# A feed-forward layer in fp32: seven-product schemes moved from every pair of its second product to all of the first and half of the second

## The chip, the core and the metric

The kernel runs on one core of a Trainium2 chip. The metric is the device time of one execution in microseconds (us); of several runs the median is taken. Five engines matter: TensorE (PE, matrix products, which accumulate in eight banks of PSUM), VectorE (DVE), ScalarE (ACT) and GpSimd (POOL) for elementwise work, and SyncE (SP), whose queue issues every DMA of this kernel in the order in which the program gives them.

## The reference, cut to what matters

One decoder layer on 1024 tokens of width 1024: attention and RWKV mixing, then the MLP that the change rewrites, then a gated embedding. Of the MLP:

```python
f = rmsnorm(h, ffn_pre_norm[i])                                   # 1024 x 1024
f = jnp.square(jax.nn.relu(f @ w_ff_in[i])) @ w_ff_out[i]         # 1024 x 4096, then 1024 x 1024
h = h + rmsnorm(f, ffn_post_norm[i])
```

## The kernel before, in words

**Numbers.** All is fp32. TensorE works on operands split in two parts: `hi` is the value rounded by a ScalarE copy to the type fp32r, `lo` is the remainder, made by a subtraction on VectorE or GpSimd. `mm3` (L289) makes each product from three matmuls, hi·hi, hi·lo and lo·hi, each with 128 rows of contraction, 128 output rows and 512 output columns. Every operand thus costs one ScalarE copy and one subtraction, each on 128x512 or 128x1024 elements.

**Order.** PE's instructions are written in the order that a planner (`Order`, L136) works out at build time: it keeps a planned time for each engine, interleaves the dense work with "chains" of dependent work (`spawn`), and so fixes PE's order. SP's order is the program's own within the MLP (`manual_schedule` at L1587). The order on VectorE, ScalarE and GpSimd is there left to the framework's scheduler, but each engine then works its queue in that order: an instruction that waits holds up those behind it. Named buffers (`rtile`, L455, and `mtile`, L1237) have a fixed place by a tag, such as `kk` or `BK2`; a new tile of a tag waits until the last reader of the old one is done.

**Before the MLP.** `out_0` and `out_1` (L1346, L1364) are the product with w_out, eight token blocks each; each `out_1(i)` spawns a chain `mixed(i)` (L1409), which normalises the token block, transposes it on PE (`tr`, tile `tp`) and stores it, split, as operand of the MLP (`put_T`, L1391; tile `f`). The MLP's first product may read tokens 0 to 511 once `mixed(3)` is done, and tokens 512 to 1023 once `mixed(7)` is done.

**First product** (1024x1024 by 1024x4096), before: plain. The 4096 hidden columns are 32 chunks `j` of 128; a chunk has two halves of 512 tokens; a half takes 8 steps of contraction, three matmuls each, into one bank `z` (`ff1_half`, L1450), then Relu and Square on ScalarE (`ff1_evac`, L1454) into `raw_h[p]` (tile `hr`), p = j // 2. Three of the halves for the first 512 tokens run while `mixed(7)` is still under way (`ff1_first`, L1627). The weights of a chunk come by one DMA of 512 KB, one copy and one GpSimd subtraction of 128x1024 (`wload`, L313).

**Second product** (1024x4096 by 4096x1024), before: the 4096 rows of contraction are 16 pairs p of two blocks of 128. For 15 of them, the pair's product is seen as 2x2 blocks by 2x2 blocks (blocks of contraction, token halves, output halves) and made with seven products of blocks instead of eight, in the manner of Strassen and Winograd. `operands` (L1499) makes the sums and differences on GpSimd, from `raw_h` (tile `sum`) and from the weights `w2r` (tile `ws`); `split2` (L1491) splits them into tiles `duo`; `prep(n)` (L1530) calls both, two products ahead; `product(n)` (L1540) makes four groups of three matmuls in banks `bk`, and after each group VectorE adds the bank to the running total `tot`, which is 28 additions in a pair. `ff1(j)` (L1583) interleaves: 12 matmuls of the first product, then one product of the second. The last pair is made plainly at the end (`last_split`, L1464, and `ff2_last`, L1649), with weights that were split early and come back by DMA (`lw`, `lwl`). `part` (L1564) uses the time between to split later weights and to put them in DRAM (`gp`, `pkg`).

## Time and profile before

| what | value |
|---|---|
| median of 3 runs (lowest, highest) | 1776.96 us (1774.38, 1780.42) |
| the profiled execution's own time | 1773.19 us |
| its span, first to last instruction | 1771.4 us |
| MLP, from the first matmul on `f` to the first on `lw` | 982.41 to 1626.10 us |
| TensorE's mean granted clock | 0.999 |

The profile shows one execution: 1.8 us of its time lie outside the span. PE's busy time counts matmuls that overlap in the array, so a matmul's duration (0.39 us) is longer than the step from one to the next. A row of a group gives its line, engine, operation, the tile written and those read, the shape, the count, the busy sum, the mean of one in ns, and the idle time of the engine just ahead of these instructions with what ended it. Nearly all elementwise work has line 113, a helper, so that tiles tell the groups apart, and all DMA issues have line 132.

### The profile page before, as it was taken

What the parts mean: (1) busy time and instruction counts of PE and PEld (TensorE: products, weight loads), DVE (VectorE), ACT (ScalarE), POOL (GpSimd) and SP (SyncE); (2) the same over time, 40 slices, a digit from 0 to 9 for tenths busy, and PEclk for the clock granted to TensorE, in tenths of its full rate; (3) what the DMA queues carried; (4) which work ended last, traced back from release to release, by engine and by line L of the source; (5) the groups of instructions that cost most, each with busy time, mean ns of one, the idle gap of its engine ahead of it and who ended that gap; (6) DMA issues with size and microseconds to landing.
All of it is one profiled execution on the core that took longest, in us unless ns stands there. A gap on an engine that the chain in (4) does not pass through costs nothing.

```text
span 1771.4 us, 25935 instructions
## 1 busy us (share of the span) xinstructions
PE 1743.8 (98%) x10192; PEld 1423.4 (80%) x10192; DVE 1017.1 (57%) x1834; ACT 732.3 (41%) x1315; POOL 670.5 (38%) x423
## 2 busy tenths in 40 slices
PE   9999989999999999999999999999999999999998
PEld 8787877878877777778888878888788888888887
DVE  6289777776534233353735466665666566556643
ACT  5824343432344343542434434343334334333454
POOL 1344131231232323332230266666665566652311
PEclk9999999999999999999999999999999999999999
DMA  4621121212332222333524132332232232305611
GB/s 163 211 95 37 49 78 47 98 43 96 86 134 84 60 60 72 110 111 135 201 96 139 64 113 95 94 115 87 92 118 91 84 95 90 123 9 179 214 48 48
DMA packets 67132, 175.51 MB, mean 99 GB/s; under 512 B 7745, under 2 KB 8129, under 8 KB 66498
## 3 DMA queue, kind: packets, MB, share of 16 engines
q1 hardware_dynamic: 67010, 173.86, 29.6%
q8 instruction: 80, 1.31, 0.3%
q14 instruction: 42, 0.34, 0.1%
HBM read 125.20 MB, written 41.94 MB: 94 GB/s over the span
## 4 chain that ended last, share of the span: by engine, by line
PE 82%; DVE 5%; DMA 5%; ACT 3%; POOL 2%; issue 2%; SPq 0%; DVEq 0%; ACTq 0%; POOLq 0%
PE z L294 18%; PE z L296 18%; PE z L292 18%; PE bk L292 6%; PE bk L294 5%; PE bk L296 5%; PE sc L275 1%; DVE xy L113 1%; PE y L275 1%; PE po L275 1%; PE pt L283 1%; PE A L275 1%; PE wr L275 1%; PE fq L275 1%; POOL wl L113 1%
## 5 line engine op out<-in xcount | busy, mean ns | idle before, releaser
L113 POOL TENSOR_TENSOR wl<-wr,wh 128x1024 fp32r<-128x1024 f32 (+1 forms) x87 | 208.0, 2392 | 431.4 <-ACT wh L113 412.2
L113 DVE TENSOR_TENSOR tot<-tot,bk 128x512 f32<-128x512 f32 x420 | 272.7, 682 | 129.9 <-PE bk L296 129.7
L292 PE MATMUL z<-uh,wh 128*128 128x512 f32 (+1 forms) x800 | 312.3, 390 | 5.5 <-ACT part L113 3.0
L296 PE MATMUL z<-uh,wl 128*128 128x512 f32 (+1 forms) x800 | 312.6, 391 | 2.7 <-POOL wl L113 2.7
L294 PE MATMUL z<-ul,wh 128*128 128x512 f32 (+1 forms) x800 | 313.6, 392 | 1.3 <-DVE ul L113 1.3
L292 PE MATMUL z<-f,wh 128*128 128x512 f32 x496 | 193.2, 389 | 0.3 <-ACT f L113 0.3
L294 PE MATMUL z<-f,wh 128*128 128x512 f32 x496 | 193.1, 389 | 0.2 <-DVE f L113 0.2
L296 PE MATMUL z<-f,wl 128*128 128x512 f32 x496 | 193.0, 389 | 0.0
L292 PEld LDWEIGHTS z<-uh,wh 128*128 128x128 f32 x800 | 151.1, 189 | 36.2 <-ACT part L113 3.5
L296 PEld LDWEIGHTS z<-uh,wl 128*128 128x128 f32 x800 | 151.0, 189 | 34.1 <-POOL wl L113 4.0
L294 PEld LDWEIGHTS z<-ul,wh 128*128 128x128 f32 x800 | 151.2, 189 | 32.3 <-issue 3.6
L292 PE MATMUL bk<-duo 128*128 128x512 f32 x420 | 164.3, 391 | 4.0 <-DVE tot L113 3.9
L294 PE MATMUL bk<-duo 128*128 128x512 f32 x420 | 163.5, 389 | 0.0
L296 PE MATMUL bk<-duo 128*128 128x512 f32 x420 | 163.5, 389 | 0.0
L113 ACT ACTIVATE wh<-wr 128x1024 fp32r<-128x1024 f32 (+1 forms) x87 | 90.3, 1038 | 119.0 <-PE z L294 89.8
L113 POOL TENSOR_TENSOR duo<-w2r,duo 128x512 fp32r<-128x512 f32 x45 | 66.7, 1483 | 166.0 <-ACT duo L113 166.0
L113 POOL TENSOR_TENSOR duo<-ws,duo 128x512 fp32r<-128x512 f32 x60 | 81.0, 1350 | 122.3 <-ACT duo L113 119.0
L292 PEld LDWEIGHTS z<-f,wh 128*128 128x128 f32 x496 | 93.1, 188 | 20.0 <-ACT f L113 0.5
L294 PEld LDWEIGHTS z<-f,wh 128*128 128x128 f32 x496 | 93.1, 188 | 19.8 <-DVE f L113 0.5
L296 PEld LDWEIGHTS z<-f,wl 128*128 128x128 f32 x496 | 93.1, 188 | 19.2
L292 PEld LDWEIGHTS bk<-duo 128*128 128x128 f32 x420 | 78.8, 188 | 23.7 <-DVE tot L113 7.0
L296 PEld LDWEIGHTS bk<-duo 128*128 128x128 f32 x420 | 78.8, 188 | 16.4
(312 smaller groups left out, 3203.5 us busy)
## 6 DMA issues: line engine op xcount, KB each, us to landing
wr<-in_wz_dram SPq DMA_DIRECT2D x48, 512.0 KB, 3.7
wr<-in_wff_dram SPq DMA_DIRECT2D x31, 512.0 KB, 3.6
w2r<-in_w_ff_dram SPq DMA_DIRECT2D x30, 512.0 KB, 4.2
xt<-in_x_dram SPq DMA_DIRECT2D x16, 512.0 KB, 4.3
gscr<-gst SPq DMA_DIRECT2D x32, 256.0 KB, 2.0
g<-gscr SPq DMA_DIRECT2D x16, 512.0 KB, 4.2
wpg<-pkg SPq DMA_DIRECT2D x16, 512.0 KB, 6.7
sw<-qk SPq DMA_DIRECT2D x48, 128.0 KB, 2.3
```

The costliest lines, as they stand in the source:

```text
L113: return f(*a, **kw)
L275: PE.matmul(out_, a, b, start=start, stop=stop)
L283: PE.transpose(out_, a, ident if idn is None else idn)
L292: PE.matmul(ps, ah, bh, start=start and i == 0, stop=False, skip_group_check=not start)
L294: PE.matmul(ps, ah, bl, start=False, stop=False, skip_group_check=not start)
L296: PE.matmul(ps, al, bh, start=False, stop=i == n - 1, skip_group_check=not start)
```

## The change

**First product: sevens everywhere.** Contraction halves by token halves, and a pair of 128-column chunks, form the 2x2 blocks. Seven products per pair, each four steps of contraction (12 matmuls, `w1_mm`), replace four chunk halves of 24 matmuls. The operand sums on the token side are made once, in `put_f` (tiles `F[1]` to `F[7]`, for tokens 512 to 1023 six POOL operations in a block where there were none). The sums of weights are made for each pair on GpSimd (`w1_sum`, four), after 256 KB loads (`w1_raw`).

**Two of the seven made first.** Products 1 and 2 of a pair need only the first 512 tokens. All 32 of them (`early`) come ahead: 27 before anything that needs tokens 512 to 1023, five interleaved with pair 0. Their results go to DRAM (`p1_scr`, `c_scr`) and come back with four 256 KB loads for each pair (`take`). The other five (`SEQ`, function `first`) accumulate in two banks `z`, taken in turn; VectorE adds the bank to `raw_h`.

**Second product: sevens for even pairs only.** `seven` is the old `product` with a new order (`MUL`); `plain` makes odd pairs with eight products, where both blocks of contraction add up in the bank (six matmuls for each VectorE addition, 16 additions in a pair). In even pairs the operand sums of `raw_h` move from GpSimd to VectorE, and the subtractions of their splits from VectorE to GpSimd. The four sums of weights for an even pair are made and split during the odd pair before (`w2_sums`), written to DRAM (`bs_scr`, 512 KB each) and loaded again in `prep`.

**Order and rooms.** Subtractions are put off by a few matmuls (`pend`, `flush`). Between products of the second stand 2 or 3 `chunks` of three matmuls of the first. Buffers change tags: `tot` lies in the old place of `f`, three tags rotate for `w2r`, and the late loads (`e_weights`, `last_split`, `last_weights`) come at other points of the last pair.

```diff
+        yield from put_f(hh, i)
...
+    def put_f(srcs, i):
...
+        if i == 4:
+            for n, p, h in ((3, 0, 0), (7, 1, 0), (5, 0, 1), (6, 1, 1)):
+                t = mtile("hl"[p], h, [128, 2, 4, 512], "f", F32R)
+                F[n] = t[:, 0], t[:, 1]
+            F[4] = [rtile([128, 4, 512], "f", tag, F32R) for tag in ("AR0", "AR1")]
...
+                S.activation(at(1 + b, 0), ps, AF.Copy)
+                V.tensor_tensor(at(1 + b, 1), ps, at(1 + b, 0), OP.subtract)
...
+        t2, t4 = (rtile([128, 4, 128], n, tag) for n, tag in (("t2", "pg"), ("t4", "yc")))
+        V.tensor_tensor(t2, d, at(1, 0), OP.add)
+        V.tensor_tensor(t2, t2, at(1, 1), OP.add)
+        G.tensor_tensor(c, c, at(1, 0), OP.subtract)
+        G.tensor_tensor(c, c, at(1, 1), OP.subtract)
+        G.tensor_tensor(t4, at(2, 0), t2, OP.subtract)
+        G.tensor_tensor(t4, t4, at(2, 1), OP.add)
+        for n, x, eng in ((7, d, V), (6, t2, V), (5, c, G), (4, t4, G)):
+            S.activation(at(n, 0), x, AF.Copy)
+            eng.tensor_tensor(at(n, 1), x, at(n, 0), OP.subtract)
...
-    MUL = (2, 1, 6, 5, 3, 7, 4)
+    MUL = (1, 6, 5, 3, 7, 4, 2)
     INTO = {1: (0, 0), 6: (1, 0), 5: (1, 1), 3: (0, 1), 7: (1, 1), 4: (1, 0), 2: (0, 0)}
-    FIRST = (2, 1, 7)
+    FIRST = (1, 7, 2)
...
-            tot.append(mtile("hl"[m], 1, [128, 2, 4, 512], f"tot{m}", F32))
+            t = rtile([128, 2, 4, 512], "tot", GA[m])
+            tot.append([t[:, 0], t[:, 1]])
...
+    SEQ = (6, 5, 7, 3, 4)
...
+    p1_scr, c_scr = ([dram.tile([128, 512], F32, name=f"{n}scr{p}") for p in range(NP)] for n in ("p1", "c"))
+    bs_scr = {(p, i): dram.tile([128, 2, 512], F32, name=f"bs{p}_{i}") for p in range(0, NP - 1, 2) for i in (6, 5, 7, 4)}
...
+    def w1_split(j):
+        if j >= len(prods):
+            return
+        k, p, i = prods[j]
+        src = w1_slot(p, {6: 11, 5: "s1", 7: 21, 3: 12, 4: 22}[i]) if k is None else A_["raw"][:, k % 4]
+        w = w1_tile(j)
+        S.activation(w[:, 0], src, AF.Copy)
+        lo = lambda: (V if j < NA and j % 4 == 3 else G).tensor_tensor(w[:, 1], src, w[:, 0], OP.subtract)
+        lo() if j < NA else pend.append(lo)
...
+    def w1_mm(j, ps, start):
+        w, f = w1_tile(j), F[prods[j][2]]
+        return mm3(ps, [(w[:, 0, c * 128:c * 128 + 128], w[:, 1, c * 128:c * 128 + 128], f[0][:, c, :], f[1][:, c, :])
+                        for c in range(4)], start)
...
+    def early(j):
...
+        if i == 1:
+            A_[p] = bank()
+        ps = A_[p]
+        yield from w1_mm(j, ps, i == 1)
+        dst = A_["out"][:, k % (4 if k < NA else 2)]
+        if i == 1:
+            S.activation(dst, ps, AF.Copy)
+        else:
+            S.activation(dst, ps, AF.Relu)
+            S.activation(dst, dst, AF.Square)
+        SY.dma_start((p1_scr if i == 1 else c_scr)[p], dst)
...
+            w1_sum(p + 1, 2)
+        if n == 4:
+            w1_sum(p + 1, 4)
+        if n < 2:
+            W1["ps", n] = zbank()
+        ps = W1["ps", n % 2]
+        yield from w1_mm(j, ps, n < 2)
+        x = raw_h[p][:, {6: 1, 5: 3, 7: 3, 3: 1, 4: 2}[i]]
+        V.tensor_tensor(x, x, ps, OP.add)
+        if i in (7, 3, 4):
+            S.activation(x, x, AF.Relu)
+            S.activation(x, x, AF.Square)
+    Y = {"j": NA, "g": None, "n": 0}
...
+    def mlp():
+        last["turn"] = tc.manual_schedule(engines={mybir.EngineType.SP})
+        last["turn"].__enter__()
+        while sch.t < t_f.get(3, 1e9):
+            yield 0.0
+        for j in range(NA):
+            beside(j)
+            yield from early(j)
+        while sch.t < t_f.get(7, 1e9):
+            yield 0.0
+        for n in range(5):
+            beside(NA + 2 * n)
+            yield from chunks(4 * n + 4)
+            beside(NA + 2 * n + 1)
+            Y["j"] += 1
+            yield from early(NA + 2 * n + 1)
+            flush()
+        prep(0)
+        prep(1)
+        flush()
+        for p in range(1, NP):
+            Y["n"] = 0
+            e = p - 1
+            if e % 2 == 0:
+                for x in range(7):
+                    yield from chunks((20 * x + 23) // 7 if p < NP - 1 else (3, 6, 9, 13, 17, 20, 20)[x])
+                    yield from seven(items.index((e, x)))
+                    if x == 0:
+                        load_w2(p)
+                    if x == 4:
+                        take(p + 1)
+                    if p == NP - 1:
+                        if x in (1, 2, 5):
+                            e_weights((1, 2, 5).index(x))
+                        if x == 5:
+                            last_split(0, (0, 1), (0,))
+                            last_split(1, (1, 0), (1,))
+                continue
+            for u in range(8):
+                yield from chunks((20 * u + 23) // 8)
+                if u == 0:
+                    load_w2(p)
+                yield from plain(items.index((e, u // 2)), u % 2)
+                if u == 1:
+                    take(p + 1)
+                    w2_sums(p, 0)
+                if 0 < u < 6:
+                    w2_sums(p, u)
+                part(2 * p - 4 + u // 2, u % 2)
+        flush()
...
     def load_w2(p):
         if p == NP - 1:
             return
-        if p % 2 == 0:
-            raw_w[p] = [rtile([128, 1024], "w2r", t) for t in ("r", "k")]
-        else:
-            t = rtile([128, 2, 1024], "w2r", "BK2")
-            raw_w[p] = [t[:, 0], t[:, 1]]
-        for k in range(2):
+        raw_w[p] = [rtile([128, 1024], "w2r", ("r", "k", "MP")[(2 * p + k) % 3]) for k in range(2)]
+        for k in (0, 1):
             SY.dma_start(raw_w[p][k], w_ff2[(2 * p + k) * 128:(2 * p + k + 1) * 128, :])
...
-        eng.tensor_tensor(d[:, 1], t, d[:, 0], OP.subtract)
+        pend.append(lambda: eng.tensor_tensor(d[:, 1], t, d[:, 0], OP.subtract))
         return d
...
+    def w2_sums(p, n):
+        if p not in raw_w:
+            return
+        b = w_blocks(p)
+        if n == 0:
+            ops["t"] = [rtile([128, 512], "sum", x) for x in ("pg", "yc")]
+        t1, t2 = ops["t"]
+        if n == 0:
+            G.tensor_tensor(t1, b[1], b[0], OP.subtract)
+            G.tensor_tensor(t2, b[3], t1, OP.subtract)
+            return
+        if n == 3:
+            G.tensor_tensor(t1, b[3], b[1], OP.subtract)
+            G.tensor_tensor(t2, b[2], t2, OP.subtract)
+            return
+        x = n - 1 - (n > 3)
+        d = split2((t2, t1, t1, t2)[x], rooms(p)[1][x % 2], G)
+        if p == 0:
+            flush()
+            SY.dma_start(bs_scr[p, (6, 5, 7, 4)[x]], d.bitcast(F32))
+        else:
+            pend.append(lambda: SY.dma_start(bs_scr[p, (6, 5, 7, 4)[x]], d.bitcast(F32)))
...
+    items = [(e, x) for e in range(NP - 1) for x in range(4 if e % 2 else 7)]
     def prep(n):
-        p, i = n // 7, MUL[n % 7]
-        if p >= NP - 1:
+        if n >= len(items):
             return
-        a, b = operands(p, i)
-        duo[n] = (split2(a, ("Ep", "En", "a")[n % 3], V),
-                  split2(b, ("kk", "MP", "px")[n % 3], G))
+        e, x = items[n]
+        if e % 2 == 0:
+            i, room = MUL[x], rooms(e)[x % 3]
+            a = split2(operand(e, i), room[0], G)
+            if i in (2, 1, 3):
+                b = split2(w_blocks(e)[{2: 2, 1: 0, 3: 3}[i]], room[1], G)
+            else:
+                b = rtile([128, 2, 512], "duo", room[1], F32R)
+                SY.dma_start(b.bitcast(F32), bs_scr[e, i])
+            duo[n] = a, b
+            return
+        m, c = 1 - x // 2, x % 2
+        if c == 0:
+            room = rooms(e - 1)[2 - m]
+            duo[e, m] = [split2(raw_h[e][:, 2 * j + m], room[j], V) for j in range(2)]
+        if m == 1:
+            if c == 0:
+                ops["w"] = [rtile([128, 2, 1024], "ws", t, F32R) for t in ("BT", "BK2")]
+            hi, lo = ops["w"]
+            for j in range(2):
+                o = (slice(None), j, halves[c])
+                S.activation(hi[o], raw_w[e][j][:, halves[c]], AF.Copy)
+                pend.append(lambda o=o, j=j: G.tensor_tensor(lo[o], raw_w[e][j][:, halves[c]], hi[o], OP.subtract))
...
+    def seven(n):
+        p, x = items[n]
+        i = MUL[x]
         prep(n + 2)
         a, b = duo.pop(n)
...
         for t in range(4):
             ts = slice(t * 128, t * 128 + 128)
             if i in FIRST:
-                chain[t] = bank(("s1", "s2", "s3", "m0", "m1"))
+                chain[t] = bank(XB)
             yield from mm3(chain[t], [(a[:, 0, ts], a[:, 1, ts], b[:, 0], b[:, 1])], i in FIRST)
-            if p == 0 and i in (2, 6, 5, 3):
-                V.tensor_copy(tot[m][:, c, t], chain[t])
+            if p == 0 and i in (1, 6, 5, 3):
+                V.tensor_copy(tot[m][c][:, t], chain[t])
             else:
-                V.tensor_tensor(tot[m][:, c, t], tot[m][:, c, t], chain[t], OP.add)
+                V.tensor_tensor(tot[m][c][:, t], tot[m][c][:, t], chain[t], OP.add)
+            flush()
...
+    def plain(n, part):
+        e, x = items[n]
+        if part == 0:
+            prep(n + 2)
+        m, c = 1 - x // 2, x % 2
+        a, (hi, lo) = duo[e, m], ops["w"]
+        for t in (2 * part, 2 * part + 1):
+            ts = slice(t * 128, t * 128 + 128)
+            ps = bank(XB)
+            yield from mm3(ps, [(a[j][:, 0, ts], a[j][:, 1, ts], hi[:, j, halves[c]], lo[:, j, halves[c]])
+                                for j in range(2)])
+            V.tensor_tensor(tot[m][c][:, t], tot[m][c][:, t], ps, OP.add)
+            flush()
...
+        t = rtile([128, 2, 1024], "pe", ("BT", "BK2", "AR0", "UV")[n], F32R)
         SY.dma_start(t.bitcast(F32), pk[1][:, n])
...
-                    for p in range(2)]
+        P["wpg"] = [[mtile("hl"[p], 1 - c, [128, KT, 512], "wpg", F32R) for c in range(2)] for p in range(2)]
         P["g3"] = rtile([128, D], "g3", "v")
         SY.dma_start(P["g3"], gains[3:4, :].to_broadcast([128, D]))
```

306 lines of the change are left out of this document (173 added, 133 removed).

## The prediction

> **What bounds the kernel now.** I read the page first: the clock, the busy shares and the chain that ended last.
>
> ```profile
> span 1771.4 us, 25935 instructions
> ...
> PE 1743.8 (98%) x10192; PEld 1423.4 (80%) x10192; DVE 1017.1 (57%) x1834; ACT 732.3 (41%) x1315; POOL 670.5 (38%) x423
> ...
> PEclk9999999999999999999999999999999999999999
> ...
> PE 82%; DVE 5%; DMA 5%; ACT 3%; POOL 2%; issue 2%; SPq 0%; DVEq 0%; ACTq 0%; POOLq 0%
> ```
>
> PE is busy for 98% of the span at full clock and carries 82% of the chain: time goes only if PE gets fewer matmuls or waits less. Next comes the timeline of PE where the MLP begins.
>
> ```profile
> 980.82 0.39 PE L296 MATMUL z<-wo,mt 128*128 128x512 f32 x1
> ...
> 982.41 0.39 PE L292 MATMUL z<-f,wh 128*128 128x512 f32 x1
> ...
> 984.90 0.39 PE L296 MATMUL z<-f,wl 128*128 128x512 f32 x1
> ```
>
> From 980.82 to 984.90 lie 18 steps: one matmul costs 4.08/18 = 0.2267 us. PE passes from w_out to the MLP without a gap. Then the groups by line and shape, and PE's waits in the MLP (985 to 1630 us):
>
> ```profile
> L292 PE MATMUL z<-f,wh 128*128 128x512 f32 x496 | 193.2, 389 | 0.3 <-ACT f L113 0.3
> L292 PE MATMUL bk<-duo 128*128 128x512 f32 x420 | 164.3, 391 | 4.0 <-DVE tot L113 3.9
> ```
>
> ```profile
> L292 PE MATMUL z<-f,w 128*128 128x512 f32 x16 | 6.3, 395 | 0.0
> ```
>
> ```profile
> PE bk L292 <- DVE tot L113: 3.9, 4, 1.7
> PE z L292 <- ACT f L113: 0.3, 1, 0.3
> PE z L294 <- DVE f L113: 0.2, 1, 0.2
> ```
>
> Each count stands under three lines (hi·hi, hi·lo, lo·hi). So the MLP's products before its last pair are 3 x (496 + 16) + 3 x 420 = 1536 + 1260 = 2796 matmuls, 633.8 us, and PE waits only 3.9 + 0.3 + 0.2 = 4.4 us in all of it. The other engines do not bind, as the stretch of 13 whole pairs shows (columns: length, then busy time and count of PE, PEld, DVE, ACT, POOL, clock, DMA share, GB/s):
>
> ```profile
> 960.00:992.00 32.00, 32.00 (x159) 26.73 (x158) 24.77 (x57) 17.81 (x53) 0.48 (x1) 1.00 0.45 152
> ...
> 1063.00:1594.00 531.00, 528.35 (x2327) 435.98 (x2326) 326.03 (x479) 206.76 (x338) 328.13 (x218) 1.00 0.28 91
> ```
>
> A pair takes 531/13 = 40.8 us (180 x 0.2267). VectorE and GpSimd are busy 61% and 62% of it.
>
> **The change, part 1: matmuls.** First product: 16 pairs x 7 products x 12 = 1344 instead of 1536. Second: 8 even pairs x 84 + 7 odd pairs x 96 = 1344 instead of 1260. Sum: -192 + 84 = -108 matmuls, -108 x 0.2267 = **-24.5 us**, all on the path, since PE sets it. Transposes, the last pair and what follows keep their matmuls.
>
> **Part 2: what each engine must do in a pair.** Prices are these groups' means, and one tile's least, median and longest:
>
> ```profile
> L113 DVE TENSOR_TENSOR tot<-tot,bk 128x512 f32<-128x512 f32 x420 | 272.7, 682 | 129.9 <-PE bk L296 129.7
> ...
> L113 POOL TENSOR_TENSOR duo<-ws,duo 128x512 fp32r<-128x512 f32 x60 | 81.0, 1350 | 122.3 <-ACT duo L113 119.0 <-PE bk L296 3.2
> ...
> L113 POOL TENSOR_TENSOR ws<-w2r 128x512 f32<-128x512 f32 x30 | 47.0, 1569 | 11.2 <-PE tp L283 5.5 <-DMA w2r<-in_w_ff_dram 3.0 <-PE bk L296 0.8
> ...
> L113 DVE TENSOR_TENSOR duo<-hr,duo 128x512 fp32r<-128x512 f32 x45 | 40.6, 901 | 0.4 <-ACT duo L113 0.4
> ...
> L113 ACT ACTIVATE duo<-sum 128x512 fp32r<-128x512 f32 x60 | 36.2, 628 | 134.8 <-POOL sum L113 93.2 <-issue 30.4 <-POOL duo L113 10.5
> ```
>
> ```profile
> L113 POOL TENSOR_TENSOR duo<-ws,duo x49: 1279/1295/1764, 1100.4 to 1593.2; 128x512 fp32r<-128x512 f32 x49
> ...
> L113 DVE TENSOR_TENSOR duo<-hr,duo x36: 681/692/1712, 1118.7 to 1578.4; 128x512 fp32r<-128x512 f32 x36
> ```
>
> A pair now lasts 60 + 84 matmuls = 32.6 us if even and 60 + 96 = 35.4 us if odd. In both, GpSimd makes 5 subtractions and 4 sums for the first product. Even adds 7 + 3 split subtractions: 19 operations, 19 x 1.35 = 25.7 us (79%). Odd adds 4 for the weights, 4 sums and 4 splits staged ahead: 21 x 1.35 = 28.4 us (80%), with the 1.57 of the sums 33.0 us (93%). VectorE in an even pair: 28 + 5 additions from PSUM x 0.682 = 22.5, and 4 sums x 0.90 = 3.6: 26.1 us (80%). In an odd one: (16 + 5) x 0.682 + 4 x 0.90 for the splits + 4 x 0.90 for `part` = 21.5 us (61%). ScalarE: 27 operations at most x 0.63 = 17.0 of 35.4 us. So no engine binds on average and operands are made two products ahead, 2 x (12 + 8.6) x 0.2267 = 9.3 us. What hides the new work is 20% of slack on GpSimd instead of 38%. Waits of the kind that cost 4.4 us today stay; I add **+2 us** for the fuller queues (bounds: -4.4, if the new order of the banks frees these too, to +8, three times today's). The old waits are the nearest row, so I stay near them.
>
> **Part 3: the opening.** The 27 early products take 27 x 12 x 0.2267 = 73.4 us, beside `mixed(4..7)`. Today these chains keep PE waiting 0.5 us (the two rows of `f` above); 73 us of early products cover them altogether. But now the early products need ScalarE and GpSimd at once. ScalarE is 17.81/32 = 56% busy with `mixed` and the products' split and evacuation add 2.5 x 0.63 in each 2.72 us, 58%: over 100% as long as chains come at today's pace, so that they must spread. GpSimd, nearly idle there today (0.48 us of 32), gets 21 subtractions of weights and 4 x 6 operations of `put_f`: 45 x 1.30 to 1.76 = 58 to 79 us. In the mean it fits, at the long end it is 6 us over. A run of six `put_f` operations, 7.8 to 10.6 us, stands in GpSimd's queue ahead of subtractions that PE needs within three products, 8.2 us: 0 to 2.4 us of wait for each of four blocks. `F[5]`, `F[6]` and `F[4]` also lie where `out_1(7)` still reads, so copies of `put_f(4)` may hold ScalarE's queue until PE is through with it; three splits are made ahead, which covers 8 us. Bounds 0 to 16 (6 + 4 x 2.4); most rows lie nearer the short price (median 1.30), so I take **+5 us**.
>
> [...]
>
> **Part 4: the staged weights and SP.** Rows of DMA (KB each, median us from issue to landing), of SP's waits in the same stretch, and of the end:
>
> ```profile
> w2r<-in_w_ff_dram SPq DMA_DIRECT2D x24, 512.0 KB, 4.0
> ```
>
> ```profile
> SPq L132 <- POOL wl L113: 250.4, 23, 20.7
> ```
>
> ```profile
> wpg<-pkg SPq DMA_DIRECT2D x16, 512.0 KB, 6.7
> ...
> lw<-pkl SPq DMA_DIRECT2D x2, 512.0 KB, 3.8
> lwl<-pkl SPq DMA_DIRECT2D x2, 512.0 KB, 4.6
> pe<-pke SPq DMA_DIRECT2D x1, 1024.0 KB, 6.3
> ```
>
> ```profile
> 1612.73 0.33 SPq L132 DMA_DIRECT2D lwl<-pkl  x1
> ...
> 1618.13 0.32 SPq L132 DMA_DIRECT2D lwl<-pkl  x1
> ```
>
> ```profile
> 1626.10 0.39 PE L292 MATMUL bk<-lw,lh 128*128 128x512 f32 x1
> ```
>
> An even pair loads 4 x 512 KB in `prep`, 9.3 us ahead; a load takes 4.0 us, 6.7 in a crowd. Hidden, cost 0 (bounds 0 to the third rival). The traffic rises from about 91 GB/s: an odd and an even pair together move 2 x 3 MB of loads, 2 x 2 MB through `bs_scr` and some writes, about 10 MB in 68 us, 150 GB/s; the row of 960:992 shows 152 GB/s with PE never idle. `take` and `w1_raw` stand on SP behind waits for GpSimd, with 10 us or more until use.
>
> **Part 5: the end.** Today the two `lwl` loads of the last pair are issued at 1612.73 and 1618.13 us, 13 and 8 us ahead of their first use at 1626.10. In the new order `last_split` comes after the sixth product of the last even pair, T being its start. The 1 MB of `e_weights(2)` waits for the first product's last read of `F[4]`, at about T; behind it on SP come `lw`, then the `lwl` that goes to `kk`, which the sixth product reads until T + 2.7, then the other `lw` and `lwl`, at about T + 3.9. Landing takes 4.6 us, 6.7 in a crowd: T + 8.5 to T + 10.6. PE has 24 matmuls from T, 5.4 us, and three of the last pair: 6.1 us. It waits 2.4 to 4.5 us; **+3 us**. Nothing hides it, PE's order being fixed.
>
> **The sum.** 1773.2 (profiled execution) - 24.5 + 2 + 5 + 3 = 1758.7. The median of the runs shown is 3.8 us above the profiled execution (1776.96 - 1773.19), so the forecast is 1758.7 + 3.8 = **1762.5 us**, range of this case 1753 to 1769.
>
> **Rivals.** *No new waits* (all of -24.5, the 4.4 us go too, only the end costs 2.4): 1773.2 - 24.5 - 4.4 + 2.4 + 3.8 = 1750.5. For it: every lead (9.3 us) is twice its transfer; against it: GpSimd at 80%.
>
> *GpSimd and VectorE block each other in the opening* and PE pays the upper bound of part 3, 16 us, instead of 5: 1762.5 + 11 = 1773.5, no change that can be measured. For it: the opening puts 45 GpSimd operations beside VectorE's fullest stretch (24.77 of 32 us). Against it: medians of 1295 and 692 ns in a stretch where both are 60% busy.
>
> *Slower: SP's one queue delivers the staged weights late.* SP waited 250.4/23 = 10.9 us on a GpSimd subtraction at a time, harmless today since nothing behind it was urgent. A staged load held for 10.9 us lands 10.9 + 4.0 - 9.3 = 5.6 us late. There are 8 x 4 = 32 such loads; if one in each even pair, 8 x 5.6 = 44.8 us: 1762.5 + 44.8 = 1807. It decides from 14.5/32 = 0.45 us of mean lateness on. Against it: the new queue's waits ahead of a staged load are for rooms that fall free one product earlier.
>
> **How the numbers follow.** A measurement of this kernel can tell about 0.3%, 5.3 us, from no change. Chances: forecast 0.52, no new waits 0.21, blocking in the opening 0.10, late staged weights 0.12 (0.02 of it mild enough to stay level), other surprises 0.05 (0.02 level, 0.03 slower). Faster: 0.52 + 0.21, plus 0.03 from mild blocking, 0.76; level 0.07 + 0.02 + 0.02 = 0.11; slower 0.10 + 0.03 = 0.13. The range takes in the first two cases and the blocking one: 1748 to 1777. What it leaves out is the slower rival.
>
> **What would show it.** PE's count falls from 10192 to 10084 (some records may miss). PE's waits in the opening, on `f` weights' subtractions by GpSimd, sum to about 5 us; waits on `bk` to 4 to 7 us; one wait of about 3 us on a DMA ahead of the first matmul of `lw`. GpSimd is about 80% busy in the MLP, VectorE 80% in even pairs. A DMA from `bs` as releaser of PE or a POOL share over 93% would prove the forecast wrong, as would a wait of over 10 us before the first half's 27 products end.

## The result, and the profile after

| | before | after |
|---|---|---|
| median of the runs (lowest, highest) | 1777.09 us, 4 runs (1774.38, 1780.42) | 1834.93 us, 4 runs (1833.30, 1840.89) |
| profiled execution, its span | 1773.19, 1771.4 us | 1833.30, 1831.5 us |
| MLP, first matmul on `f` to first on `lw` | 982.41 to 1626.10: 643.7 us | 991.05 to 1681.48: 690.4 us |
| from there to the end of the span | 145.3 us | 150.0 us |

The change makes the kernel slower: ratio 1.0331, 95% interval 1.0302 to 1.0360. The forecast had been 1762.5. The page of the changed kernel, with the lines that answer to those shown of before:

```profile
span 1831.5 us, 26360 instructions
...
PE 1750.2 (96%) x10084; PEld 1415.8 (77%) x10084; DVE 1022.3 (56%) x1799; ACT 758.0 (41%) x1377; POOL 759.1 (41%) x532
...
PEclk9999989999999999999999999999999999999999
...
PE 64%; DMA 10%; DVE 7%; POOL 7%; ACT 6%; issue 4%; SPq 1%; ACTq 0%; POOLq 0%; DVEq 0%
```

PE has 108 matmuls fewer (10084 for 10192), as meant, and yet a longer busy time; its share of the chain fell from 82% to 64%. Those 18 points went to what feeds it: DMA from 5% to 10%, GpSimd from 2% to 7%, ScalarE from 3% to 6%, VectorE from 5% to 7%, the rest to SP and issue. The five largest rows of PE's waits from 985 to 1690 us of the changed kernel (all waits of the MLP together summed to 4.4 us before):

```profile
PE bk L292 <- ACT pa L113: 19.4, 6, 5.2
PE bk L292 <- DVE tot L113: 17.6, 11, 3.9
PE bk L292 <- ACT duo L113: 7.8, 4, 2.8
PE bk L292 <- ACT wh L113: 2.0, 2, 1.7
PE bk L292 <- DMA lw<-pkl: 1.9, 2, 1.0
```

Are the helpers full? Stretches of the changed kernel (length, busy time and count of PE, PEld, DVE, ACT, POOL, clock, DMA share, GB/s): the opening, two whole pairs, and the stretch of 531 us shown of before:

```profile
991.00:1064.00 73.00, 56.93 (x229) 44.79 (x229) 40.46 (x40) 37.30 (x74) 54.08 (x36) 0.88 0.36 123
1205.00:1280.00 75.00, 69.25 (x301) 56.08 (x301) 47.98 (x68) 27.80 (x48) 52.00 (x41) 1.00 0.54 186
1063.00:1594.00 531.00, 499.62 (x2131) 403.54 (x2130) 295.39 (x424) 208.48 (x358) 372.86 (x290) 0.98 0.55 190
```

No. In two pairs, 75 us for 68.0 us of matmuls (300 x 0.2267), GpSimd is busy 69% and VectorE 64%. PE waits although each of these engines has some 30% of its time to spare.

**Where the 60.1 us went** (span against span). Ahead of the MLP 8.6 us, which I count as chance: PE's work there is unchanged, and in a run of before's own code (p2 below) the MLP starts at 989.97; in e1 to e16 it starts between 984.1 and 993.6. In the MLP 46.7 us. After it 4.7 us. The MLP's 46.7, from every matmul's start: the matmuls at 0.2267 us each 636.4 to 611.9 (-24.5); PE's waits 4.4 to 52.0 (+47.6); steps much longer than 0.2267, 1.4 to 21.4 (+20.0); steps a little longer, 1.5 to 5.1 (+3.6). The trace's granted clock tells what most of the long steps are: in the changed kernel's MLP it falls to a half for eleven periods of 3.4 us, and the matmuls inside these cost 16.7 us more than at full clock; in the MLP of before it never falls.

**The opening.** The longest wait of PE there, 5.22 us, ends at 1002.80. The timeline of GpSimd, VectorE, ScalarE, SP and PE of the changed kernel around it (start, duration, engine, line, operation, shape, count, and in brackets the idle time before and what ended it):

```profile
997.74 1.59 POOL L113 TENSOR_TENSOR t<-t,f 128x512 f32<-128x512 f32 x1
...
1002.69 1.73 POOL L113 TENSOR_TENSOR c<-c,f 128x512 f32<-128x512 f32 x1 [1.35 <-DVE d L113]
1004.38 1.72 POOL L113 TENSOR_TENSOR wh<-wa,wh 128x512 fp32r<-128x512 f32 x1
1006.07 1.74 POOL L113 TENSOR_TENSOR c<-c,f 128x512 f32<-128x512 f32 x1
...
1004.89 1.76 DVE L113 TENSOR_TENSOR t<-d,f 128x512 f32<-128x512 f32 x1
1006.58 1.77 DVE L113 TENSOR_TENSOR f<-d,f 128x512 fp32r<-128x512 f32 x1
1008.27 1.77 DVE L113 TENSOR_TENSOR t<-t,f 128x512 f32<-128x512 f32 x1
...
999.37 0.63 ACT L113 ACTIVATE f<-t 128x512 fp32r<-128x512 f32 x1 [2.77 <-POOL t L113]
...
1002.16 0.58 ACT L113 ACTIVATE pa<-bk 128x512 f32<-128x512 f32 x1
...
1014.67 0.63 ACT L113 ACTIVATE f<-t 128x512 fp32r<-128x512 f32 x1 [3.12 <-POOL t L113]
1015.21 0.58 ACT L113 ACTIVATE pa<-bk 128x512 f32<-128x512 f32 x1
...
992.55 22.98 SPq L132 DMA_DIRECT2D hscr<-hh  x4
1016.35 0.33 SPq L132 DMA_DIRECT2D wa<-in_wff_dram  x1
...
1002.80 0.79 PE L292 MATMUL bk<-f,wl 128*128 128x512 f32 x1 [5.22 <-ACT pa L113]
1015.84 0.51 PE L292 MATMUL bk<-f,wh 128*128 128x512 f32 x1 [2.44 <-ACT pa L113]
```

Three things stand together. For a while GpSimd and VectorE run in turn: both start every 1.7 us and both take 1.72 to 1.77 us, for 1.295 and 0.692 in the medians shown of before. ScalarE's copies `f<-t` wait 2.77 and 3.12 us for GpSimd, and the evacuations `pa<-bk`, which free the banks that PE wants, stand behind them; PE goes on at 1002.80 and 1015.84. And SP's queue is held from 992.55 to 1015.5 by four stores of the chains, with the load of `wa`, the next early products' weights, behind them. Of GpSimd's 35 operations of 128x512 from 991 to 1064 us, 16 took 1.67 to 1.80 us; of the 40 in the two pairs shown (1205 to 1280), two did.

**The pairs.** Most waits come two at a time, where an odd pair gives way to an even one. One such place in the changed kernel, SP, ScalarE and VectorE, and PE's two waits:

```profile
1267.24 0.32 SPq L132 DMA_DIRECT2D duo<-bs  x1
1267.97 0.33 SPq L132 DMA_DIRECT2D gp<-in_pT_dram  x1
...
1271.52 0.63 ACT L113 ACTIVATE gph<-gp 128x512 fp32r<-128x512 f32 x1 [1.91 <-DMA gp<-in_pT_dram]
...
1272.18 0.69 DVE L113 TENSOR_TENSOR gp<-gp,gph 128x512 fp32r<-128x512 f32 x1 [2.69 <-ACT gph L113]
1272.79 0.68 DVE L113 TENSOR_TENSOR hr<-hr,z 128x512 f32<-128x512 f32 x1
1273.39 1.28 DVE L113 TENSOR_TENSOR tot<-tot,bk 128x512 f32<-128x512 f32 x2
1276.72 0.69 DVE L113 TENSOR_TENSOR sum<-hr,sum 128x512 f32<-128x512 f32 x1 [2.05 <-POOL duo L113]
...
1274.13 0.50 PE L292 MATMUL bk<-duo 128*128 128x512 f32 x1 [2.11 <-DVE tot L113]
1279.95 0.76 PE L292 MATMUL bk<-duo 128*128 128x512 f32 x1 [2.81 <-ACT duo L113]
1280.52 0.63 PE L294 MATMUL bk<-duo 128*128 128x512 f32 x1
1280.94 0.63 PE L296 MATMUL bk<-duo 128*128 128x512 f32 x1
```

The load of a `part` (`gp`) is issued only after the staged load `duo<-bs`, which itself waited until 1267.24 for its room. It lands at 1271.5; ScalarE and VectorE have the part's operations at the head of their queues and wait; VectorE's additions into `tot` stand behind, and PE's next bank is not free. After PE's second wait its steps are 0.42 us (1280.52 to 1280.94) instead of 0.2267: half clock (granted clock 0.50 from 1280.30 to 1281.40).

### The profile page after: what moved, and what is told of

It reads as the page before. It is cut to its first block, busy times and chain, and to the rows that moved or that the text cites. A ratio compares the mean times of both kernels' runs of the same rounds, so it can differ in the third digit from the quotient of the medians.

```text
span 1831.5 us, 26360 instructions
## 1 busy us (share of the span) xinstructions
PE 1750.2 (96%) x10084; PEld 1415.8 (77%) x10084; DVE 1022.3 (56%) x1799; ACT 758.0 (41%) x1377; POOL 759.1 (41%) x532
## 4 chain that ended last, share of the span: by engine, by line
PE 64%; DMA 10%; DVE 7%; POOL 7%; ACT 6%; issue 4%; SPq 1%; ACTq 0%; POOLq 0%; DVEq 0%
PE z L294 13%; PE z L296 13%; PE z L292 13%; PE bk L292 5%; PE bk L296 4%; PE bk L294 4%; DMA wr<-in_wff_dram 2%; DMA gp<-in_w_pleg_dram 1%; DMA g<-gscr 1%; POOL wr L113 1%; POOL duo L113 1%; SPq L132 1%; DVE xy L113 1%; PE A L275 1%; PE sc L275 1%
## 5 line engine op out<-in xcount | busy, mean ns | idle before, releaser
L113 POOL TENSOR_TENSOR wl<-wr,wh 128x1024 fp32r<-128x1024 f32 (+1 forms) x56 | 132.8, 2373 | 424.2 <-ACT wh L113 403.7
L113 DVE TENSOR_TENSOR tot<-tot,bk 128x512 f32<-128x512 f32 x336 | 219.1, 681 | 42.6 <-PE bk L296 42.1
L113 POOL TENSOR_TENSOR duo<-sum,duo 128x512 fp32r<-128x512 f32 x64 | 85.7, 1340 | 76.5 <-ACT duo L113 75.1
L292 PE MATMUL bk<-duo 128*128 128x512 f32 x224 | 90.6, 404 | 27.6 <-DVE tot L113 15.9
L113 ACT ACTIVATE wh<-wr 128x1024 fp32r<-128x1024 f32 (+2 forms) x94 | 81.0, 861 | 85.2 <-PE z L294 49.4
L113 ACT ACTIVATE duo<-sum 128x512 fp32r<-128x512 f32 x64 | 40.2, 628 | 180.7 <-POOL sum L113 76.5
L113 DVE TENSOR_TENSOR gp<-gp,gph 128x512 fp32r<-128x512 f32 x28 | 27.6, 986 | 135.8 <-ACT gph L113 135.8
L296 PE MATMUL bk<-duo 128*128 128x512 f32 x224 | 88.8, 396 | 1.2 <-POOL duo L113 1.2
L292 PE MATMUL bk<-ws,duo 128*128 128x512 f32 x224 | 87.7, 392 | 1.7 <-DVE tot L113 1.7
L294 PE MATMUL bk<-duo 128*128 128x512 f32 x224 | 88.6, 396 | 0.0
L296 PE MATMUL bk<-ws,duo 128*128 128x512 f32 x224 | 87.2, 389 | 0.0
L294 PE MATMUL bk<-ws,duo 128*128 128x512 f32 x224 | 87.2, 389 | 0.0
L292 PE MATMUL z<-f,wh 128*128 128x512 f32 x212 | 84.1, 397 | 1.1 <-DVE hr L113 1.0
L294 PE MATMUL z<-f,wh 128*128 128x512 f32 x212 | 83.8, 395 | 0.0
L296 PE MATMUL z<-f,wh 128*128 128x512 f32 x212 | 83.7, 395 | 0.0
L113 DVE TENSOR_TENSOR hr<-hr,z 128x512 f32<-128x512 f32 x80 | 54.4, 680 | 49.4 <-PE z L296 49.4
```

Source lines behind the costliest of these rows:

```text
L113: return f(*a, **kw)
L292: PE.matmul(ps, ah, bh, start=start and i == 0, stop=False, skip_group_check=not start)
L294: PE.matmul(ps, ah, bl, start=False, stop=False, skip_group_check=not start)
L296: PE.matmul(ps, al, bh, start=False, stop=i == n - 1, skip_group_check=not start)
```

## The experiments

The changed kernel is the base unless another is named; each ratio is to runs of before taken with that kernel. Waits are PE's, in us, in the one profiled execution (in three profiles of before's own code, before, p1 and p2, the pairs have 2.2, 0.2 and 3.7): "opening" in the first 143 us from the first matmul on `f`, with the pairs' start, "pairs" from there to the first matmul on `lw`.

| kernel | median us | ratio to before (95%) | opening | pairs |
|---|---|---|---|---|
| after | 1834.93 | 1.0331 (1.0302, 1.0360) | 19.4 | 31.6 |
| e1 | 1823.30 | 1.0254 (1.0227, 1.0281) | 9.7 | 32.6 |
| e2 | 1818.40 | 1.0229 (1.0205, 1.0252) | 19.0 | 24.6 |
| e3 | 1804.50 | 1.0149 (1.0125, 1.0173) | 10.7 | 24.2 |
| e4 | 1842.61 | 1.0352 (1.0320, 1.0383) | 19.6 | 40.2 |
| e5 | 1856.28 | 1.0451 (1.0415, 1.0487) | 33.6 | 33.2 |
| e6 | 1842.72 | 1.0374 (1.0343, 1.0404) | 25.2 | 32.7 |
| e7 | 1797.80 | 1.0107 (1.0066, 1.0148) | 3.9 | 24.4 |
| e8 | 1846.28 | 1.0397 (1.0364, 1.0429) | 25.9 | 30.7 |
| e9 | 1800.96 | 1.0138 (1.0110, 1.0166) | 4.8 | 21.9 |
| e10 | 1799.43 | 1.0136 (1.0105, 1.0166) | 4.5 | 25.6 |
| e11 | 1807.72 | 1.0171 (1.0145, 1.0197) | 5.7 | 27.8 |
| e12 | 1807.04 | 1.0171 (1.0140, 1.0202) | 5.1 | 28.1 |
| e13 | 1795.19 | 1.0114 (1.0089, 1.0138) | 8.4 | 15.9 |
| e14 | 1799.05 | 1.0130 (1.0099, 1.0161) | 6.9 | 18.9 |
| e15 (leaves work out) | 1774.74 | 0.9996 (0.9981, 1.0010) | 7.9 | 3.0 |
| e16 (leaves work out) | 1774.83 | 0.9987 (0.9972, 1.0002) | 8.0 | 6.8 |

### e1 to e3: the opening's GpSimd work, and the place of the parts

e1 puts the six GpSimd operations of `put_f` on VectorE:

```diff
-        G.tensor_tensor(c, c, at(1, 0), OP.subtract)
+        V.tensor_tensor(c, c, at(1, 0), OP.subtract)
...
-        for n, x, eng in ((7, d, V), (6, t2, V), (5, c, G), (4, t4, G)):
+        for n, x, eng in ((7, d, V), (6, t2, V), (5, c, V), (4, t4, V)):
```

> Theory: PE's 19.4 us of waits in the opening come from ScalarE's queue, where copies of the operand sums wait for GpSimd and VectorE, which block each other, ahead of the evacuations that PE needs. With the six GpSimd operations of put_f on VectorE, the waits on the evacuations fall below 5 us, four or five of the 3.4 us periods at half clock go with them, and the time falls by about 25 us, to 1810. Rival: ScalarE simply has too much to do there; its work is unchanged, so the waits stay near 19 us and the time near 1835.

The opening's waits fell from 19.4 to 9.7 us, the time by 11.6. Half of the expectation: two long waits stayed (5.5 and 4.1 us). Both end with an evacuation `pa` on ScalarE: the first while SP is held for 14.6 us by the four stores, with `wa` behind them; the second behind a copy that waits 4.2 us for GpSimd's sum of pair 0's weights. Whether the gain comes from the end of the alternation or from VectorE's shorter operations was not told apart.

e2 issues the load of a part before `prep` issues its staged load:

```diff
+                if u % 2 == 0:
+                    part(2 * p - 4 + u // 2, 0)
...
                 yield from plain(items.index((e, u // 2)), u % 2)
...
-                part(2 * p - 4 + u // 2, u % 2)
+                if u % 2:
+                    part(2 * p - 4 + u // 2, 1)
```

> Theory: the two waits at each change from an odd to an even pair (32 us in all) come from one chain on SP's queue: a staged load waits for its room, the load of the later weights is issued behind it, VectorE's queue stops at the subtraction that needs that load, and the next staged load is issued behind the stores of its result. With that load issued ahead of the staged one, these waits fall from 32 to about 12 us, four of six half-clock periods go, and the time falls by about 24 us, to 1811. Rival: GpSimd and VectorE are too full in the pairs; the order on SP changes nothing, 1835 within 5.

Waits in the pairs 31.6 to 24.6, half-clock periods there 5 to 2, the time down by 16.5 us. The place is a cause; but the waits did not fall to 12, they moved: now "POOL duo", about 2.1 us each, in the middle of the even pairs.

e3 joins both, and puts the last of `e_weights` behind `last_split`:

```diff
-                        if x in (1, 2, 5):
-                            e_weights((1, 2, 5).index(x))
+                        if x in (1, 2):
+                            e_weights((1, 2).index(x))
...
                             last_split(1, (1, 0), (1,))
+                            e_weights(2)
```

> Both edits, and in the last pair the 1 MB load issued behind the last pair's weights instead of ahead of them. Theory: the parts add up, 1835 - 25 - 24 - 2 = 1784, still slower than 1777. Rival: the waits move on to other places once these are gone, and less than half of the 51 us comes back, 1810 or more.

The two gains add (11.6 + 16.5 = 28.1 of 30.4 us), and the tail's waits stay at 3.2. But 1804.5 lies far above the 1784 of the theory, and just short of the rival's 1810, with 30.4 of the hoped-for 51 us: more causes than two.

### e4: is GpSimd too full?

The four subtractions that split an odd pair's own weights (`ws`) go to VectorE:

```diff
-                pend.append(lambda o=o, j=j: G.tensor_tensor(lo[o], raw_w[e][j][:, halves[c]], hi[o], OP.subtract))
+                pend.append(lambda o=o, j=j: V.tensor_tensor(lo[o], raw_w[e][j][:, halves[c]], hi[o], OP.subtract))
```

> Only the four subtractions for the weights of an odd pair move from GpSimd to VectorE (28 operations of 1.3 us in all). Theory (SP's queue decides in the pairs): no change, 1835 within 5, the two waits at each change of pair stay. Rival (GpSimd is late): the waits in the pairs fall by 10 us or more, to 1820 or less.

Less work for GpSimd did not help, so that the rival falls. The waits of the profiled execution grew to 40.2 us, but that was the slowest of the four runs (1846.69), and the ratio's interval overlaps that of the changed kernel: that four more operations in VectorE's queue, which the parts still held up, hurt is not shown.

### p1 and p2: what a wait costs beyond itself

Both are the kernel before, with 24 times 24 matmuls and a pause behind its last output; in p1 a pause is two ScalarE copies between two transposes, in p2 three more.

```diff
+            for n in range(24):
...
+                yield from mm3(ps, [(w[0][1][:, k, 0:128], w[1][1][:, k, 0:128], w[0][1][:, k, :], w[1][1][:, k, :])
+                                    for k in range(KT)])
...
+                S.activation(z[:, 0:128], q[:, 0:128], AF.Copy)
+                for _ in range(chain):
+                    S.activation(z[:, 0:512], z[:, 0:512], AF.Copy)
...
+                tr(q[:, 0:128], z[:, 0:128], 0.107)
```

> The kernel before, with work added behind its last output: 24 times 24 matmuls and then a pause, in which PE waits for a transpose to go through two short ScalarE copies and come back; its output is the kernel's own. Theory (the clock is halved for a 3.41 us period when PE idled more than half of the period before): pauses of about 1.1 us leave the clock full, so that the added stretch takes 24 x (24 x 0.2267 + 0.2 + 1.1) = 162 us. Rival (the half-clock periods do not hang on idle time): the same here.

> The same with three more ScalarE copies of 128x512 in each pause, about 1.6 us longer, 2.7 us in all. Theory: four in five of the pauses are followed by a half-clock period, each of which costs up to 1.7 us more: 24 x 1.6 + 20 x 1.4 = 66 us more than with the short pauses. Rival: 24 x 1.6 = 38 us more, at full clock.

The same stretch of p1 and then of p2 (the column before the last two is the granted clock):

```profile
1775.00:1930.00 155.00, 130.75 (x575) 102.07 (x574) 0.00 (x0) 19.95 (x44) 0.00 (x0) 1.00 0.00 0
```

```profile
1775.00:1930.00 155.00, 109.35 (x383) 84.26 (x381) 2.71 (x6) 41.40 (x76) 0.00 (x0) 0.83 0.01 4
```

and PE's waits in it, of p1 and of p2 up to the end (total, times, longest; with its first pause, ahead of 1775 us, p1 has 24 that sum to 26.4):

```profile
PE z L283 <- ACT pz L113: 25.3, 23, 1.4
```

```profile
PE z L283 <- ACT pz L113: 73.9, 24, 3.4
```

The pauses of 1.1 us left the clock at 1.00; those of 3.1 us brought it to 0.83, each followed by a stretch of half clock of 3.4 us, twice of 6.8, in which a matmul's step is about doubled, as at 1280.52 above (0.42 for 0.2267 us). Time 1937.15 and 2026.02 (two runs each, 1.4 and 6.1 us apart): 88.9 us between them for 47.5 us more of waiting (73.9 - 26.4), so that each long pause cost another 1.7 us (41.4/24). In the changed kernel's MLP eleven such periods follow its waits: 11 x 1.7 = 18.7 us, against the 16.7 counted from its matmuls (PE is idle through most of one of the periods). In the changed kernel the periods begin on one grid of 3.4 us (at 1200.94, 1279.44 and 1426.22, for instance, 23 and 43 steps apart), and PE's idle time within a step of that grid tells what follows: from the MLP's start to 8 us past its end, all 12 steps with 1.79 us or more were followed by half clock, and none with 1.70 us or less. In all 20 traces together the border after a step at full clock lies between 1.6 and 1.9 us; after a step at half clock about 0.7 us were enough to keep it there (p2, at 1865.30 and 1971.11). So a step of which PE idled little more than half, 1.79 of 3.4 us, was enough.

### e5, e6, e8: the program's own order on every engine

In the MLP the framework's scheduler orders the queues of VectorE, ScalarE and GpSimd. e5 is the changed kernel, e6 is e3 and e8 is e7 (below), each with the program's order there instead:

```diff
-        last["turn"] = tc.manual_schedule(engines={mybir.EngineType.SP})
+        last["turn"] = tc.manual_schedule(engines=OTHERS)
```

> The changed kernel with VectorE, ScalarE and GpSimd held to the program's own order in the MLP, as SP is, where the framework's scheduler had put work of later products ahead. Theory: the waits in the pairs come from such work at the head of a queue (splits for the next pair that wait for a load, ahead of operands that PE needs); they fall from 32 us to 12 or less, and with the half-clock periods behind them the time falls by 25 us or more, to 1810 or less. Rival: SP's one queue and the rooms decide, whatever the order elsewhere; the waits in the pairs stay over 24 us.

> The three earlier edits together (operand sums on VectorE, the later weights' load ahead of the staged one, the 1 MB load last) and the program's own order. Theory: waits in the pairs below 8 us, 1804 - 20 = 1784 or less. Rival: no less than 1800.

> All of these edits and the program's own order on all engines. Theory: both gains add up, 1791 - 20 = 1771, below the kernel before; with no waits left at all the count of matmuls alone gives 1777 - 24.5 = 1753. Rival: waits move on, 1785 or more.

All are slower than with the scheduler's order, by 21, 38 and 48 us, and the theory fails in all three. The opening gets waits of 13.6 to 19.4 us in one piece, and most even pairs begin with one of 1.6 to 2.8 us: VectorE's operand sums wait there for the last Relu and Square of the pair (`hr`), and the additions into `tot` stand behind them. In e5 a second wait follows in most even pairs, on the staged load `duo<-bs` itself: 13.4 of the 33.2 us. Going back to the program's own order is thus no cure: it has waits of its own.

### e7: the rest of the opening

On e3: the last four chains' stores go to ScalarE's DMA queue, and the sums and splits of pair 0 run on VectorE.

```diff
-            SY.dma_start(h_scr[i][:, halves[c]], hh[c])
+            (nc.scalar if i > 3 else SY).dma_start(h_scr[i][:, halves[c]], hh[c])
...
+        G = V if p == 0 else GP_
```

> The three earlier edits, the stores of the chains for tokens 512 to 1023 issued on ScalarE's DMA queue instead of SP's, and the sums of pair 0's weights on VectorE, which idles there. Theory: the two waits left in the opening are a load of weights held on SP's queue behind a store that waits for its chain (5.5 us), and ScalarE's split of a staged sum that waits for GpSimd (4.8 us); both go, the opening's waits fall from 10.7 to 3 us or less, three half-clock periods go, 1804 - 8 - 5 = 1791. Rival for the first: ScalarE's own load; then at least 5 us of the waits stay.

The opening is down to 3.9 us: of its 19.4, `put_f` on GpSimd makes about ten (e1), and the stores in SP's queue and pair 0's sums, which were moved together here, most of the rest. The pairs did not move.

### e9 to e12: two places in the even pairs

In e7's trace most even pairs show one wait of 0.6 to 1.9 and one of 2.0 to 2.2 us. Ahead of the second GpSimd runs the four `ws` subtractions in one piece, then the `duo<-sum` that PE needs:

```profile
1409.56 5.05 POOL L113 TENSOR_TENSOR ws<-w2r,ws 128x512 fp32r<-128x512 f32 x4
1414.56 1.28 POOL L113 TENSOR_TENSOR wr<-wr 128x512 f32<-128x512 f32 x1
1415.79 1.26 POOL L113 TENSOR_TENSOR duo<-sum,duo 128x512 fp32r<-128x512 f32 x1
```

e9 gives two sums rooms of their own, e10 moves the `ws` subtractions to VectorE (as e4 did), e11 does both, e12 is e9 with half of them moved (`V if j else G`); all on e7.

```diff
-            ops["a", 3] = rtile([128, 512], "sum", "ex")
+            ops["a", 3] = rtile([128, 512], "sum", "pg")
...
-            ops["a", 7] = rtile([128, 512], "sum", "py")
+            ops["a", 7] = rtile([128, 512], "sum", "yc")
```

> The kernel of e7 with one edit: in even pairs the sums for the third and seventh product of blocks get rooms of their own (tags pg and yc) instead of the rooms of the sums before them (ex and py). In e7's trace VectorE stands 2.24 us (ended by POOL duo) before sum<-hr,sum, its additions into tot stand behind that, and PE waits 1.6 to 1.9 us in the middle of an even pair (1178.93, 1251.95, 1326.93, 1400.65, 1547.48, 1620.57). Theory, single rooms of the sums: these six waits go, with some short ones; PE's waits in the pairs fall from 24.4 to about 13 us, the time by some 11 us, 1787. Rival, the additions are late for another reason (ScalarE's copies, the clock): the waits stay and the time is 1798, as e7's.

> The kernel of e7 with one edit: the four subtractions that split an odd pair's own weights (ws) run on VectorE instead of GpSimd. In e7's trace GpSimd does all four in one stretch of 5.05 us, ahead of duo<-sum, the subtraction that PE waits for 2.0 to 2.2 us at the end of each even pair (1195.51, 1269.23, 1343.30, 1417.11, 1489.85, 1564.78). e4, the same move on the changed kernel alone, made the waits longer, but there VectorE's queue was held by the parts. Theory, the burst on GpSimd: six waits of 2.1 us and three half-clock periods of 1.7 us go, about -15 to -18 us, 1781. Rival, VectorE's additions become late in their place as in e4: waits in the pairs of 24 us or more, time 1798 or more.

> Both edits, of e9 and of e10. If both theories hold and nothing else is next: waits in the pairs below 4 us, all half-clock periods in the pairs gone, 1798 - 11 - 17 = 1770, 0.4 to 0.5% below the kernel before. If the two waits stand for one lack of slack, one edit's gain eats the other's: 1780 or more.

> e9's edit, and of the four subtractions of ws only two on VectorE, the other two left on GpSimd: its burst is 2.5 us instead of 5.05, VectorE gets 1.4 us less than in e11. If the length of the burst sets the wait, 2.1 us becomes none, as it exceeds the lead by only 2.1: about e11's time, or below it if VectorE is short of time in e11. If any burst there costs: half of it, some 7 us above e11.

Each wait aimed at went or shrank, and about the same sum came back elsewhere: 21.9 to 28.1 us for e7's 24.4, and no time is clearly below e7's. So the theories of e9 to e11 missed, and e10 and e11 came out as their rivals had it. e12, at e11's time, agrees with the first of its two cases, but by luck: its waits did not go, they are of 3.7 to 4.1 us on `tot`. In e11 it is one wait of 4.2 to 4.8 us in most even pairs. What stands before it, ScalarE, VectorE, SP and PE of e11:

```profile
1404.38 2.38 ACT L113 ACTIVATE ws<-w2r 128x512 fp32r<-128x512 f32 x4 [6.60 <-DMA w2r<-in_w_ff_dram]
...
1405.04 1.28 DVE L113 TENSOR_TENSOR ws<-w2r,ws 128x512 fp32r<-128x512 f32 x1 [5.46 <-ACT ws L113]
1406.24 2.47 DVE L113 TENSOR_TENSOR tot<-tot,bk 128x512 f32<-128x512 f32 x4
...
1397.27 0.91 SPq L132 DMA_DIRECT2D w2r<-in_w_ff_dram  x2
...
1407.01 0.76 PE L292 MATMUL bk<-duo 128*128 128x512 f32 x1 [4.66 <-DVE tot L113]
```

The scheduler has put the next odd pair's split `ws` into the queues here, right behind the issue of its load. The load lands late, and whatever stands behind the split waits with it: on ScalarE if the copies come first, on VectorE or GpSimd through the subtractions. That is why mending one queue showed the wait in another.

### e13, e14: the load earlier

On e11 and e9: the `w2r` load is issued at the start of the even pair's phase, ahead of the `w1_raw` loads that hold SP.

```diff
+                load_w2(p)
                 for x in range(7):
...
-                    if x == 0:
-                        load_w2(p)
```

> The kernel of e11 with one edit: in the phase of an even pair the loads of the odd pair's weights (w2r) are issued at the phase's start, ahead of the loads of w1_raw, instead of after the first product of blocks. In e11's trace SP issues them at 1397.27 behind three wr loads, which waited until 1395.46 for GpSimd; ScalarE's split ws<-w2r, which the scheduler has put early, then waits 6.60 us for them, VectorE's ws<-w2r waits 5.46 us for ScalarE with additions into tot behind it, and PE waits 4.66 us. Theory, a late load in front of a hoisted split: the loads land some 4 to 5 us earlier, waits in the pairs fall from 27.8 to below 10 us, the half-clock periods go too, and the time is 1775 to 1782. Rival, the two pairs' cycle has one limit elsewhere, since e7, e9, e10 and e11 all give 4 to 4.7 us of waiting in two pairs whatever is edited: waits again 22 to 28 us, time 1797 or more.

> The kernel of e9 (the four subtractions of ws on GpSimd) with the same earlier loads. By the theory of the late load the small waits on POOL duo and DMA go, but GpSimd's burst of 5.05 us ahead of duo<-sum stays: waits of 2.1 us at seven places, 15 us in all, time about 1790. By the rival nothing changes: 22 us, 1800.

On e11, waits in the pairs 27.8 to 15.9, the ratio 1.0171 to 1.0114. Half right: a burst of four copies and four subtractions still stands in the middle of the even pair (2.3 to 3.9 us of wait, once 1.0), and PE now waits 4.2 us for pair 0's staged load. In time e13 is level with e7 (1.0107), from which its edits started. e14 keeps 18.9 us of waits and gives e9's time within its interval.

### e15, e16: the burst, or too little slack?

e15 is e13 without the burst: only the first odd pair splits its weights, and all odd pairs use them. e16 is e13 without the staging: only pair 0's sums of weights are made and stored, and all even pairs load them; this takes 10.8 us (8 x 1.35) of GpSimd's work out of two pairs but leaves the burst.

```diff
-            if c == 0:
+            if c == 0 and e == 1:
                 ops["w"] = [rtile([128, 2, 1024], "ws", t, F32R) for t in ("BT", "BK2")]
             hi, lo = ops["w"]
-            for j in range(2):
+            for j in range(2 if e == 1 else 0):
```

```diff
-        if p not in raw_w:
+        if p:
             return
...
-                SY.dma_start(b.bitcast(F32), bs_scr[e, i])
+                SY.dma_start(b.bitcast(F32), bs_scr[0, i])
```

> The kernel of e13, and of all odd pairs only the first splits its weights (ws); the others use that pair's split weights again. It leaves out 24 ScalarE copies, 24 VectorE subtractions and nothing of PE's work, loads or stores, so its output is not the reference's. In e13's trace the four copies and four subtractions of ws run in one burst in the middle of an even pair (ScalarE 1399.23 to 1402, VectorE 1400.35 to 1403.3) and PE waits 2.3 to 2.9 us there (3.9 once). Theory, it is the burst that the scheduler pulls ahead into the queues: the six or seven waits go, the waits in the pairs fall from 15.9 to about 5 us (the first even pair's 5.05 on duo<-bs stay), with the half-clock periods beside them the time falls by 14 to 18 us, to about 1779. Rival, the helpers lack slack in the mean and any work taken off helps in proportion: 1.4 us of VectorE's 48 in two pairs, 3%: waits of 13 us or more, time above 1789.

> The kernel of e13, and only pair 0's sums of weights are made, split and stored; all even pairs load those. It leaves out 28 GpSimd sums, 28 ScalarE copies, 28 GpSimd subtractions and 28 stores of 512 KB, all in odd pairs, so its output is not the reference's; the loads stay. Theory, the burst of ws in the even pair: the waits there stay, 12 to 16 us in the pairs, time 1788 to 1796. Rival, lack of slack in the mean: GpSimd loses 10.8 of its 52 us in two pairs, a fifth, more than e15 takes off any engine, so that the waits fall below 8 us and the time to 1780 or less.

PE's waits from 1130 to 1610 us, of e13, of e15 and of e16:

```profile
PE bk L292 <- ACT duo L113: 11.5, 5, 2.9
PE bk L292 <- issue: 3.9, 1, 3.9
PE bk L292 <- DVE tot L113: 0.4, 2, 0.2
```

```profile
PE bk L294 <- POOL duo L113: 2.7, 5, 0.7
PE bk L292 <- DMA duo<-bs: 0.2, 1, 0.2
```

```profile
PE bk L292 <- issue: 6.8, 6, 1.8
```

That e16 still has the burst, its ScalarE and VectorE show:

```profile
1313.35 2.18 ACT L113 ACTIVATE ws<-w2r 128x512 fp32r<-128x512 f32 x4
...
1314.48 3.00 DVE L113 TENSOR_TENSOR ws<-w2r,ws 128x512 fp32r<-128x512 f32 x4
```

Without the burst 15.8 us become 2.9 and the ratio falls from 1.0114 to 0.9996, 1795.19 to 1774.74 us: e15's expectation for the burst held. But without the staging they become 6.8, with the burst still there, and the time 1774.83 us, which is what the rival had said. So both are needed for the 15.8 us: with either one gone most of them go. A reading that fits, but was not tested, is that a burst of some 3 us makes PE wait when the queues are late already, and that the staging, in the pair before, makes them late. Which of the staging's parts matters was not told apart: operations, stores, or traffic (166 GB/s in e16 for 188 in e13, from 1130 to 1580 us).

## Why the prediction was wrong, step by step

**Part 1** was right: 108 matmuls fewer, -24.5 us at full clock.

**Part 2 is the step that failed.** "So no engine binds on average and operands are made two products ahead" is true and did not carry its "+2 us": the waits in the pairs rose from 2.2 to 31.6 us. GpSimd was even less full than forecast (69% for 80%). What the step left out is the order in the queues: an operation that waits for a late load stands ahead of one that PE needs. e2 (the parts) and e13 (the `w2r` load) took out 7 and 12 us, each from its own base, without taking any work away; e15 took out 13 with the burst. But the amount of work is not without effect: e16 left the burst where it was and took out 9 us with the staging. The bound of +8, "three times today's", scaled the waits of a kernel without staged loads, in whose whole MLP PE waited four times for `tot`.

**Part 3** named the right engines and missed the size: the opening's waits rose by 17.2 us (2.2 to 19.4), above its upper bound of 16. GpSimd was not full: 54.1 of 73 us, for 58 to 79 forecast. Its operations did not keep "the short price" where they met VectorE's: there those of both engines took 1.7 to 1.8 us from start to end. That is less than one operation after the other would take: each engine started one every 1.7 us, where the two medians of before make 1.295 + 0.692 = 1.99. And PE did not wait for GpSimd itself: all 19.4 us are waits for ScalarE's evacuations, which in the two places shown stood behind copies that waited for GpSimd, and e7 shows that stores in SP's queue or pair 0's sums held the opening too, which no step had.

**Part 4** costed staged loads and SP at 0. In the changed kernel the staged loads did come in time (0.2 us of waiting on `bs`), so the slower rival's mechanism was not this one; e5 shows that it can be. The step asked whether a staged load is late and not what stands behind it on SP: the parts' loads. The traffic came to 186 GB/s in two pairs, not 150, and `w2r`, issued behind three loads of `wr` and a staged one, took 6.4 us to land instead of 4.2 (medians of the two kernels).

**Part 5** was right: 3.3 us of waits on `lw` and `lwl` for +3, and one half-clock period.

**What no step had** is the clock. In p2 a wait that was followed by a half-clock period cost 1.7 us more; with 47.6 us of new waits came 16.7 us of matmuls at half clock. Of the gap between forecast and profile, 1833.3 - 1758.7 = 74.6 us, the waits of the MLP make 47.6 - 7 = 40.6, its longer steps 23.6 (16.7 of them at half clock), its start 8.6, the rest of the tail 1.7 (4.7 - 3).

Of the signs that were to prove the forecast wrong, only one appeared, and it was of no weight: PE waited 0.2 us on `bs`. GpSimd's share stayed far below 93%, and no wait reached 10 us. No sign looked at what stands behind a waiting operation.

**Where the gain goes even when the pairs run well.** e15 ties with before. Its MLP is 12.1 us shorter (643.7 to 631.6), not 24.5: 7.9 us of waits in the opening and on pair 0's first staged load, three half-clock periods, 3.0 in the pairs, against 4.4 before. Its tail is 6.1 us longer, and its MLP begins 4.6 later, within the spread of the starts. No kernel here that does all the work beats the one before.

## What to carry to other kernels

Busy shares and leads say whether the work fits, not whether it arrives in time: for every operation that a change adds, list what stands behind it in its engine's queue and in the DMA queue, and what late thing it may itself be waiting for. Several such waits hide behind each other, so mending one shows little until the last is gone; leaving the suspected work out altogether told more than moving it. And a wait of PE above 3 us should be costed at its length plus the 1.7 us of p2: in all traces here 66 of 68 such waits that began at full clock (24 of them p2's pauses) were followed by half clock, of those between 2 and 2.25 us 13 of 29.
